# An RWKV-7 recurrence: values centred beforehand, a norm over whole tiles, and the log decay summed in two halves

## The chip, the cores and the metric

The kernel runs on one core of a Trainium2 chip. Its engines are TensorE (PE; its weight loads are listed apart as PEld), VectorE (DVE), ScalarE (ACT), GpSimd (POOL) and SyncE (SP), which issues most transfers. Each engine works through its own instructions in the order in which they stand. The metric is the device time in microseconds (us), lower is better. A profile of one execution is available for each kernel.

## What is computed

The reference is a trunk of two layers over 256 frames of width 2048: RWKV-7 time mixing, a SwiGLU, forgetting attention, a SwiGLU, and a last norm. The change touches the RWKV-7 layer alone, with 32 heads of 64 channels:

```python
w_log = -softplus(-(w0 + tanh(xw @ w1) @ w2)) - 0.5
decay = exp(-exp(w_log))
...
S_t = S_{t-1} diag(w_t) + (S_{t-1} a_t) b_t^T + v_t k_t^T          # per head
y_t = S_t r_t
...
mu = mean(y, axis=-1); var = mean(square(y - mu), axis=-1)          # over a head's 64 channels
y = (y - mu) * rsqrt(var + GN_EPS) * lnx_g + lnx_b
y = y + sum(r * k * r_k, axis=-1) * v                               # the bonus
return (y * g) @ w_o
```

The state is linear in the values: if the mean over a head's 64 channels is taken from each `v_t`, the outputs `y_t` come out with mean zero.

## The kernel before, in words

All large products go through a stream of weights. SP loads `st` (128 x 1024), ACT rounds each 128x512 block to a high half `wh` (line 149), DVE subtracts to get the low half `wl` (line 150), and PE multiplies three times per block and row tile (lines 182 to 184, the "main" matmuls). The inputs are halved in the same way, so that three products in the reduced 32-bit format stand for one in full 32 bits.

Work that isn't such a product is written as Python generators. After each triple of main matmuls the stream takes one step of each active generator (`tick`), so that recurrence work lies between main matmuls. A scheduler then orders the instructions of each engine by their dependences and places buffers.

The RWKV-7 layer has a stage of keys, a stage of values (`v0` to `v3`, about 157 to 252 us in the profile; its results go to DRAM as `vdram`), and the recurrence stage (about 252 to 615 us) under the products for the receptance, the decay, the gates and the output. There are eight units: four groups of eight heads by two row tiles of 128 frames, each of two chunks of 64 frames. For each unit
- `prepare` turns the decay `tw` into cumulative log decays with a triangular matmul (line 571), exponentials of them (lines 586 to 590 and 599), scaled keys, transposes (lines 635 and 649, copied out at lines 643 and 654), and the chunk matrices `M` (matmul line 665, masked on DVE at line 668);
- `solve` and `merge` invert a triangular block (lines 692 to 780; matmuls at 742, 749, 759, 775);
- `chain` carries the state through the two chunks (matmuls at 820, 823, 829, 834, 836; values loaded as `sv` and `vu` by `values`);
- `post` norms the result: sum per head (line 858), squares about the mean in eight ACT steps of 64 columns with a running sum (line 867), a power on POOL (line 870), the bonus from the two chunks' `vu` (line 876), the normalising in eight ACT steps (line 882), gain, bonus and gate (lines 883 to 888), and transposes (line 896).

`tw` is made at line 946 by a tanh on ACT and at line 947 by a scale and offset on DVE. The vu buffers are four, sv two. The triangular matmul is the only one of 512 columns that runs in full 32 bits.

Of the kernel before, what the change touches and what calls it, by code (L numbers as in the profile page):

```python
# [8 lines left out]
F32 = mybir.dt.float32  # L9
# [24 lines left out]
C_ID, C_TRI, C_IND, C_M, C_E, C_B8, C_LANE, C_I8, C_CAUSAL, C_END = 0, 128, 256, 258, 386, 450, 482, 486, 550, 678  # L34
# [7 lines left out]
def constants():  # L42
# [18 lines left out]
    c[:, C_CAUSAL : C_CAUSAL + P] = np.where(s[None, :] <= s[:, None], 0.0, MASKED)  # L61
    return c
# [145 lines left out]
def hybrid_kernel(ctx, tc, const, x, a_norm_g, a_mix, a_w_rkv, a_w0, a_w1, a_w2, a_a0, a_a1, a_a2,  # L208
# [127 lines left out]
    with ExitStack() as actx:  # L336
        a1 = actx.enter_context(tc.tile_pool(name="a1", bufs=1))
        rv = actx.enter_context(tc.tile_pool(name="rv", bufs=2))
        vdram = dram.tile([T, D], F32, name="vdram")
        loraw = {}  # L340

        with ExitStack() as bctx:
# [150 lines left out]

            def early():
# [29 lines left out]
            for g in range(4):  # L524
                ps = S.gemm(f"v{g}", lhs_of(xv), ready=lambda kt: has("xv", kt))
                for t in range(2):
                    vt = rv.tile([P, 512], F32, name="rv")
                    nc.scalar.copy(vt[:, :], ps[t][:, :])
                    nc.sync.dma_start(vdram[t * P : (t + 1) * P, g * 512 : (g + 1) * 512], vt[:, :])
            S.until(lambda: not S.act and not S.pend)  # L530

        with ExitStack() as bctx:
# [4 lines left out]
            u4 = bctx.enter_context(tc.tile_pool(name="u4", bufs=4))  # L537
# [5 lines left out]
            vec, wat, rts, gts, units = {}, {}, {}, {}, {}  # L543

# [17 lines left out]
            def prepare():  # L562
                for i, (g, t) in enumerate(order):
# [22 lines left out]
                    nc.scalar.activation(W, ps[:, :], AF.Exp)  # L586
                    nc.scalar.activation(Wi[:, :], ps[:, :], AF.Exp, scale=-1.0)
                    for c in range(2):
                        for q in range(2):
                            nc.scalar.activation(wc[half[c], q:8:2], pc[half[q], c:8:2], AF.Exp)  # L590
# [8 lines left out]
                    nc.scalar.activation(Wp, Wp, AF.Exp)  # L599
# [184 lines left out]
            def values(g, t, c):  # L784

                a, b = u2.tile([P, 512], F32, name="sv"), u4.tile([P, 512], F32, name="vu")
                r0 = t * P + c * C
                for d in (a, b):
                    nc.sync.dma_start(d[half[c], :], vdram[r0 : r0 + C, g * 512 : g * 512 + 512])
                return a, b  # L790

            def chain():
                nxt = values(0, 0, 0)
                for i, (g, t) in enumerate(order):
# [10 lines left out]
                    vus = []  # L805
                    for c in range(2):
# [4 lines left out]
                        vus.append(vu)  # L811
# [38 lines left out]
                    S.add(post(i, g, t, Y, vus, bon))  # L850

            def post(i, g, t, Y, vus, bon):
# [4 lines left out]
                m8 = u1.tile([P, 8], F32, name="m8")  # L857
                nc.vector.tensor_reduce(m8[:, :], h4(Y[:, :]), AX.X, ALU.add)
# [535 lines left out]
```

## Time and profile before

| | |
|---|---|
| runs (us) | 2623.15, 2628.25, 2627.87; median 2627.87 |
| the profiled execution (us) | 2622.87 |
| its span, first to last instruction (us) | 2621.1 |
| mean granted TensorE clock | 0.997 |

The profile lists for each engine the time in which it was busy. A row "A <- B" of waits names the instruction A before which its engine was idle and what released it. The chain of work that ended last is followed back from the last instruction, at each step to what released it or to the instruction ahead on its engine. Ends of matmuls are modelled, so pieces of PE work that overlap look longer than the distance between their starts.

### The profile page before, as it was taken

How to read it: one execution, taken by the hardware profiler on the slowest of the kernel's cores; microseconds unless marked ns; L12 is line 12 of the kernel's file. 1: busy time of each engine (PE TensorE's matmuls, PEld its weight loads, DVE VectorE, ACT ScalarE, POOL GpSimd, SP SyncE). 2: the span in 40 equal slices, each digit the busy share in tenths (PEclk: the TensorE clock that was granted, in tenths of full speed). 3: DMA queues.
4: the chain of work that ended last, by engine and by line, in shares of the span. 5: the costliest groups of instructions: out<-in, count | busy, mean ns of one | idle time of the engine just before them, and what ended most of it. 6: DMA issues, size and time to landing. Idle time of an engine off the chain costs nothing.

```text
span 2621.1 us, 40943 instructions
## 1 busy us (share of the span) xinstructions
PE 2574.1 (98%) x15160; PEld 2110.4 (81%) x15160; DVE 1675.0 (64%) x2965; ACT 1481.8 (57%) x2869; POOL 92.2 (4%) x69
## 2 busy tenths in 40 slices
PE   7999999999999999999999999999999999999998
PEld 5788777778888888888888888888888888888887
DVE  7885888877555555555556677676755555555554
ACT  6665787876545454544455656555554545454444
POOL 0000010100000000000001010010000000000000
PEclk9999999999999999999999999999999999999999
DMA  6676323335666666655556666664666666665554
GB/s 193 181 212 215 111 86 102 105 114 154 192 186 192 187 192 186 192 193 192 189 190 205 201 201 185 184 203 155 188 189 189 190 188 192 187 192 190 195 193 161
DMA packets 253945, 468.46 MB, mean 179 GB/s; under 512 B 22248, under 2 KB 32696, under 8 KB 253744
## 3 DMA queue, kind: packets, MB, share of 16 engines
q1 hardware_dynamic: 250448, 463.10, 58.2%
q10 hardware_dynamic: 3136, 2.74, 0.3%
q8 instruction: 119, 1.95, 0.3%
q14 instruction: 82, 0.67, 0.1%
q0 software_dynamic: 160, 0.00, 0.0%
HBM read 457.37 MB, written 4.23 MB: 176 GB/s over the span
## 4 chain that ended last, share of the span: by engine, by line
PE 92%; ACT 4%; DVE 2%; issue 1%; DMA 1%; POOL 0%; SPq 0%; POOLq 0%; ACTq 0%; DVEq 0%
PE mm L182 28%; PE mm L184 28%; PE mm L183 28%; PE bg L997 1%; ACT xb L643 1%; PE bg L829 1%; DVE wl L150 1%; PE bg L820 1%; PE bg L665 1%; PE bg L836 1%; ACT Bs L867 1%; PE bg L312 1%; PE bg L834 1%; PE bg L823 0%; DVE xmf L376 0%
## 5 line engine op out<-in xcount | busy, mean ns | idle before, releaser
L150 DVE TENSOR_TENSOR wl<-st,wh 128x512 fp32r<-128x512 f32 (+1 forms) x1648 | 1129.8, 690 | 813.1 <-ACT wh L149 806.1
L149 ACT CAST wh<-st 128x512 fp32r<-128x512 f32 (+1 forms) x1648 | 1015.8, 622 | 952.2 <-DVE wl L150 697.3
L182 PE MATMUL mm<-wh,xb 128*128 128x512 f32 x2048 | 804.6, 393 | 0.0
L184 PE MATMUL mm<-wh,xb 128*128 128x512 f32 x2048 | 800.9, 391 | 0.0
L183 PE MATMUL mm<-wl,xb 128*128 128x512 f32 x2048 | 800.5, 391 | 0.0
L182 PEld LDWEIGHTS mm<-wh,xb 128*128 128x128 f32 x2048 | 385.0, 188 | 79.5 <-issue 3.3
L184 PEld LDWEIGHTS mm<-wh,xb 128*128 128x128 f32 x2048 | 384.8, 188 | 78.8
L183 PEld LDWEIGHTS mm<-wl,xb 128*128 128x128 f32 x2048 | 385.0, 188 | 75.9
L183 PE MATMUL mm<-wl,xa 128*128 128x512 f32 x768 | 305.3, 398 | 3.0 <-DVE wl L150 1.5
L182 PE MATMUL mm<-wh,xa 128*128 128x512 f32 x768 | 306.7, 400 | 0.0
L184 PE MATMUL mm<-wh,xa 128*128 128x512 f32 x768 | 305.0, 397 | 0.0
L184 PE MATMUL mm<-wh,hb 128*128 128x512 f32 x448 | 174.5, 390 | 0.0
L183 PE MATMUL mm<-wl,hb 128*128 128x512 f32 x448 | 174.5, 390 | 0.0
L182 PE MATMUL mm<-wh,hb 128*128 128x512 f32 x448 | 174.5, 390 | 0.0
L183 PEld LDWEIGHTS mm<-wl,xa 128*128 128x128 f32 x768 | 145.2, 189 | 33.0 <-DVE wl L150 3.2
L184 PEld LDWEIGHTS mm<-wh,xa 128*128 128x128 f32 x768 | 145.0, 189 | 30.0 <-issue 0.2
L182 PEld LDWEIGHTS mm<-wh,xa 128*128 128x128 f32 x768 | 145.4, 189 | 28.8 <-issue 1.0
L182 PEld LDWEIGHTS mm<-wh,hb 128*128 128x128 f32 x448 | 84.1, 188 | 17.5
L183 PEld LDWEIGHTS mm<-wl,hb 128*128 128x128 f32 x448 | 84.1, 188 | 17.5
L184 PEld LDWEIGHTS mm<-wh,hb 128*128 128x128 f32 x448 | 84.1, 188 | 17.3
L1181 POOL TENSOR_TENSOR n<-n,pw 128x8 f32<-128x8 f32 x24 | 47.2, 1968 | 409.0 <-DVE n L1180 409.0
L1224 ACT ACTIVATE sc<-sc,nm 128x128 f32<-128x128 f32 x64 | 28.7, 449 | 26.6 <-DVE nm L1223 26.6
(293 smaller groups left out, 1941.7 us busy)
## 6 DMA issues: line engine op xcount, KB each, us to landing
st<-in_f_w_gu_dram SPq DMA_DIRECT2D x352, 512.0 KB
st<-in_f_w_d_dram SPq DMA_DIRECT2D x176, 512.0 KB
st<-in_b_w_in_dram SPq DMA_DIRECT2D x128, 512.0 KB
st<-in_a_w_rkv_dram SPq DMA_DIRECT2D x96, 512.0 KB
st<-in_a_w_o_dram SPq DMA_DIRECT2D x32, 512.0 KB
st<-in_b_w_o_dram SPq DMA_DIRECT2D x32, 512.0 KB
cb<-cdram SPq DMA_DIRECT2D x4, 1024.0 KB
x<-in_x_dram SPq DMA_DIRECT2D x12, 256.0 KB
```

The lines of the kernel that those rows point to most:

```text
L149: nc.scalar.copy(hi[:rows, :n], st)
L150: nc.vector.tensor_tensor(lo[:rows, :n], st, hi[:rows, :n].bitcast(F32), op=ALU.subtract)
L182: nc.tensor.matmul(ps[t][:, :n], xh[:rows, c], wh, start=b == 0, stop=False)
L183: nc.tensor.matmul(ps[t][:, :n], xh[:rows, c], wl, start=False, stop=False)
L184: nc.tensor.matmul(ps[t][:, :n], xl[:rows, c], wh, start=False, stop=b == kts - 1)
L312: nc.tensor.transpose(tp[:, i * T + t * P : i * T + (t + 1) * P], src[:, t, c : c + P], ident)
L643: nc.scalar.copy(dst, tpv[half[q], :, c, :])
L665: mm(pm[c][:, h * P : (h + 1) * P], fkb[us, b * 4 + h, :], far[us, b * 4 + h, :], start=True, stop=True)
L820: mm(pb[us, hs], M[:, c * 8 + h, C : 2 * C], sv[:, hs], start=True, stop=True)
L829: mm(pu[us, hs], TT[us, h, :], vu[us, hs], start=True, stop=True)
L1181: nc.gpsimd.tensor_tensor(n8[:, :], n8[:, :], pw[:, :], op=ALU.pow)
L1224: nc.scalar.activation(sc[:, c], sc[:, c], AF.Exp, bias=nm[:, t : t + 1], accum_out=nm[:, 2 + t : 3 + t])
```

## The change

Four things change in the RWKV-7 layer; nothing after it is touched.

1. While the values are made, `centred` takes each head's mean from them and writes a second copy to DRAM, `wdram`. `chain` reads the recurrence's values from `wdram`. Since `vu` is then no longer the value that the bonus needs, `post` loads the original values from `vdram` as `vn`, and `vu` has two buffers in place of four.
2. `post` needs no mean: one square over the whole tile on ACT, a sum per head on DVE, the power on POOL, and one multiplication of the whole tile on DVE in place of eight ACT steps each for squares and normalising.
3. The log decay is summed before its constant: `tw` stays the tanh, and its scale and offset move into the scale and a bias column (`dec`, four new columns of the constants) of the exponentials. Line 947 goes.
4. The triangular matmul runs as two matmuls in the reduced format, on a high half `th` (cast on ACT) and a low half `tl` (subtraction on DVE). They use the buffers named `k2` and `Wi`, which are free at that point of `prepare`.

```diff
+    n = s % C + 1
+    c[:, C_DEC : C_DEC + 4] = NEG_HALF_EXP * np.stack([n, -n, n - 1, 0 * n + C], 1)
...
+            def centred(vt, at):
+                v8 = vt[:, :].rearrange("p (h n) -> p h n", n=N)
+                m8 = lw.tile([P, 8], F32, name="m8")
+                nc.vector.tensor_reduce(m8[:, :], v8, AX.X, ALU.add)
+                nc.vector.tensor_scalar(m8[:, :], m8[:, :], -1.0 / N, None, op0=ALU.mult)
+                yield
+                wt = pre.tile([P, 2, T], F32, name="f2")[:, :, :].rearrange("p i n -> p (i n)")
+                nc.vector.tensor_tensor(
+                    wt.rearrange("p (h n) -> p h n", n=N), v8, m8[:, :].unsqueeze(2).broadcast_to([P, 8, N]), op=ALU.add
+                )
+                nc.sync.dma_start(wdram[at], wt)
...
+                    nc.sync.dma_start(vdram[at], vt[:, :])
+                    S.add(centred(vt, at))
...
+            tri = g1.tile([P, P], F32R, name="tri")
+            nc.vector.tensor_copy(tri[:, :], cst[:, C_TRI : C_TRI + P])
+            dec = cst[:, C_DEC : C_DEC + 4]
...
+                    th = u1.tile([P, 512], F32R, name="k2")
+                    tl = u1.tile([P, 512], F32R, name="Wi")
+                    nc.scalar.copy(th[:, :], tw[:, :])
+                    nc.vector.tensor_tensor(tl[:, :], tw[:, :], th[:, :].bitcast(F32), op=ALU.subtract)
                     ps = yield from S.take()
                     pc = yield from S.take()
-                    mm(ps[:, :], cst[:, C_TRI : C_TRI + P], tw[:, :], start=True, stop=True)
+                    yield
+                    mm(ps[:, :], tri[:, :], th[:, :], start=True, stop=False)
+                    mm(ps[:, :], tri[:, :], tl[:, :], start=False, stop=True)
...
-                    nc.scalar.activation(W, ps[:, :], AF.Exp)
-                    nc.scalar.activation(Wi[:, :], ps[:, :], AF.Exp, scale=-1.0)
+                    nc.scalar.activation(W, ps[:, :], AF.Exp, scale=NEG_HALF_EXP, bias=dec[:, 0:1])
+                    nc.scalar.activation(Wi[:, :], ps[:, :], AF.Exp, scale=-NEG_HALF_EXP, bias=dec[:, 1:2])
...
-                a, b = u2.tile([P, 512], F32, name="sv"), u4.tile([P, 512], F32, name="vu")
+                a, b = u2.tile([P, 512], F32, name="sv"), u2.tile([P, 512], F32, name="vu")
...
+                vn = u1.tile([P, 512], F32, name="vn")
+                nc.sync.dma_start(vn[:, :], vdram[t * P : (t + 1) * P, g * 512 : (g + 1) * 512])
...
-                for h, hs in enumerate(hsl):
-                    nc.scalar.activation(y2[:, hs], Y[:, hs], AF.Square, bias=m8[:, h : h + 1], accum_out=r8[:, h : h + 1])
+                nc.scalar.activation(y2[:, :], Y[:, :], AF.Square)
...
+                nc.vector.tensor_reduce(r8[:, :], h4(y2[:, :]), AX.X, ALU.add)
...
-                    nc.vector.tensor_tensor(
-                        h4(y2[vs, :]), h4(vus[c][vs, :]), bon[vs, :].unsqueeze(2).broadcast_to([C, 8, N]), op=ALU.mult
-                    )
+                nc.vector.tensor_tensor(h4(y2[:, :]), h4(vn[:, :]), b8(bon[:, :]), op=ALU.mult)
...
-                for h, hs in enumerate(hsl):
-                    nc.scalar.activation(Y[:, hs], Y[:, hs], AF.Identity, scale=r8[:, h : h + 1], bias=m8[:, h : h + 1])
+                nc.vector.tensor_tensor(h4(Y[:, :]), h4(Y[:, :]), b8(r8[:, :]), op=ALU.mult)
...
-                    nc.vector.tensor_scalar(a[:, :], a[:, :], NEG_HALF_EXP, NEG_HALF_EXP, op0=ALU.mult, op1=ALU.add)
```

The scheduler puts all engines' instructions into a new order. Three places follow; line numbers are those of each kernel, and of lines that both have the new numbers are 3 higher in the weight stream and 29 higher in the recurrence up to `values`.

ACT, where `post` of the first unit meets `prepare` and `merge` of later ones (Bs, r, m, Y: the norm's tiles; Xs: merge's copies; 643 and 654 `prepare`'s copies; 149 weight casts). Before:

```order
L149 CAST wh<-st 128x512
L845 COPY Y<-bg 64x512
L743 COPY Xs<-bg 128x256
L867 ACTIVATE Bs,r_3893<-Y,m_3748 128x64 x7
L743 COPY Xs<-bg 128x256
L867 ACTIVATE Bs,r_3893<-Y,m_3748 128x64
L643 COPY xb_2534<-bg 64x4x64 x8
L654 COPY WW<-bg 64x4x128 x4
```

ACT at the second unit's `post` in the changed kernel (887 the whole-tile square, 594 the cast of the high half of a later unit, 772, 672 and 683 what were 743, 643 and 654):

```order
L872 COPY Y<-bg 64x512
L973 ACTIVATE ta_4551<-mm 128x512
L887 ACTIVATE Bs<-Y 128x512
L152 CAST wh<-st 128x512
L948 COPY gt_4765<-mm 128x512
L594 CAST k_4561<-tw_4492 128x512
L152 CAST wh<-st 128x512
L772 COPY Xs<-bg 128x256
L152 CAST wh<-st 128x512
L606 ACTIVATE rr<-kk 128x512
L772 COPY Xs<-bg 128x256
L672 COPY xb_2581<-bg 64x4x64 x8
```

Eight steps ahead of the copies of `prepare` have become one, further ahead of them, and a cast has come in.

PE at the third unit's triangular matmul (665 the chunk matrices of the unit before, 759 and 775 `merge`, 820 the first matmul of `chain`). Before:

```order
L665 MATMUL bg<-xb_2535,WW 128x128 x7
L759 MATMUL bg<-Ti,xb_2534 32x32 x16
L665 MATMUL bg<-xb_2535,WW 128x128 x8
L571 MATMUL bg<-tw_3322,cst 128x512
L573 MATMUL bg<-cst,tw_3322 128x2 x4
L775 MATMUL bg<-Tt,Xs 32x32 x16
L820 MATMUL bg<-sv,xb_2534 64x64 x8
```

The same place in the changed kernel (694 was 665, 602 was 573, 804 was 775, 847 was 820; k and Wi are the high and the low half):

```order
L694 MATMUL bg<-xb_2581,WW 128x128 x11
L599 MATMUL bg<-k_3462,tri 128x512
L600 MATMUL bg<-Wi,tri 128x512
L804 MATMUL bg<-Tt,Xs 32x32 x5
L602 MATMUL bg<-cst,tw_3380 128x2 x4
L804 MATMUL bg<-Tt,Xs 32x32 x11
L186 MATMUL mm<-wl,xa_1478 128x512
L847 MATMUL bg<-sv,xb_2580 64x64 x8
```

The two matmuls stand where the one stood, with `merge` and `chain` behind them.

DVE in the changed kernel, ahead of the masks (697, formerly 668) whose results end the fifth unit's `prepare`; 595 makes the low half of the sixth unit:

```order
L595 TENSOR_TENSOR Wi<-tw_4494,k_5091 128x512
L604 TENSOR_TENSOR kk<-x_475,vk 128x512
L153 TENSOR_TENSOR wl<-st,wh 128x512 x2
L900 TENSOR_TENSOR Bs<-vn,bon 128x512
L780 TENSOR_TENSOR Ti<-bg,Ti 128x256
L901 TENSOR_TENSOR Bs<-Bs,vb 128x512
L782 STREAM_TRANSPOSE Tt<-Ti 128x256
L153 TENSOR_TENSOR wl<-st,wh 128x512
L903 TENSOR_TENSOR Y<-Y,r_5013 128x512
L697 TENSOR_TENSOR xb_2580<-bg,cst 128x512 x2
```

DVE at the same point of the first unit, where it makes the low half of the second:

```order
L697 TENSOR_TENSOR xb_2580<-bg,cst 128x512 x2
L153 TENSOR_TENSOR wl<-st,wh 97x512
L595 TENSOR_TENSOR Wi<-tw_2800,k_3059 128x512
L697 TENSOR_TENSOR xb_2580<-bg,cst 128x512 x2
L622 TENSOR_REDUCE n_3124<-rr 128x8
L614 TENSOR_TENSOR WW<-bg,tw_2800 128x512
```

And DVE before, at the masks that end the fifth unit's `prepare`:

```order
L601 SCALAR_TENSOR_TENSOR k_5212<-ta_4512,va 128x512
L751 TENSOR_TENSOR Ti<-bg,Ti 128x256
L602 SCALAR_TENSOR_TENSOR k_5212<-k_5212,x_474 128x512
L753 STREAM_TRANSPOSE Tt<-Ti 128x256
L668 TENSOR_TENSOR xb_2534<-bg,cst 128x512 x2
L869 TENSOR_SCALAR r_5047<-r_5047 128x8
L668 TENSOR_TENSOR xb_2534<-bg,cst 128x512 x2
L585 TENSOR_TENSOR WW<-bg,tw_4440 128x512
```

The subtraction is new ahead of the masks in the one unit and between them in the other, and the norm's whole-tile products (900 to 903) stand ahead of masks.

## Rows read from the trace of the kernel before

**Rows 1.** The page: span, and busy time of each engine with its share.

```profile
span 2621.1 us, 40943 instructions
...
PE 2574.1 (98%) x15160; PEld 2110.4 (81%) x15160; DVE 1675.0 (64%) x2965; ACT 1481.8 (57%) x2869; POOL 92.2 (4%) x69
```

**Rows 2.** Windows: stretch, busy PE, PEld, DVE, ACT, POOL, clock, DMA share, GB/s.

```profile
157.00:180.00 23.00, 22.42 (x122) 18.51 (x121) 19.54 (x41) 14.73 (x32) 1.59 (x5) 1.00 0.85 240
180.00:203.00 23.00, 23.00 (x103) 19.09 (x102) 11.64 (x18) 10.50 (x19) 1.59 (x1) 1.00 0.92 263
...
252.00:615.00 363.00, 347.87 (x4885) 274.96 (x4884) 291.04 (x624) 277.84 (x698) 34.95 (x25) 0.99 0.35 107
...
660.00:1400.00 740.00, 739.98 (x3338) 611.15 (x3337) 409.30 (x611) 370.10 (x612) 3.49 (x6) 1.00 0.63 190
```

**Rows 3.** Waits of PE, 250 to 645: us, times, longest; 8 of 12 rows.

```profile
PE bg L649 <- ACT xb L643: 2.7, 5, 0.8
PE bg L665 <- ACT WW L654: 2.3, 6, 1.0
PE bg L742 <- issue: 1.7, 1, 1.7
PE mm L183 <- issue: 1.5, 1, 1.5
PE bg L573 <- DVE xb L668: 1.4, 1, 1.4
PE bg L635 <- issue: 1.3, 1, 1.3
PE bg L896 <- DVE Y L888: 1.0, 1, 1.0
...
PE bg L820 <- issue: 0.3, 1, 0.3
```

**Rows 4.** The chain of work, 240 to 650 and 340 to 560: shares by line.

```profile
by line: PE mm L184 14.0%; PE mm L183 13.9%; PE mm L182 13.6%; ACT xb L643 4.5%; PE bg L829 4.2%; PE bg L820 3.7%; PE bg L665 3.7%; PE bg L836 3.6%; ACT Bs L867 3.5%; issue 3.3%; PE bg L834 3.2%; PE bg L823 3.1%; ACT WW L654 2.0%; ACT TT L7
...
by line: PE mm L184 8.9%; PE mm L182 8.7%; PE mm L183 8.4%; ACT xb L643 6.5%; PE bg L829 5.8%; PE bg L820 4.9%; PE bg L836 4.9%; PE bg L823 4.4%; ACT Bs L867 4.2%; PE bg L665 4.2%; PE bg L834 4.0%; ACT TT L769 3.6%; ACT Y L882 3.5%; issue 3
```

**Rows 5.** Timeline around 377 us: start, length, engine, instruction, idle before and releaser.

```profile
376.77 0.19 ACT L867 ACTIVATION_READ_ACCUMULATOR Bs<-Y,m 128x1 f32 x1
...
377.73 3.02 ACT L643 COPY xb<-bg 64x256 f32<-64x256 f32 x8
...
379.28 0.66 PE L649 MATMUL bg<-cst,xb 128*128 128x128 f32 x4 [0.76 <-ACT xb L643]
```

**Rows 6.** ACT groups, 252 to 615, and L1016 of the page: count | busy, mean ns.

```profile
L882 ACT ACTIVATE Y<-Y,m,r 128x64 f32<-128x64 f32 x64 | 22.4, 428 | 1.7 <-DVE m L880 1.6
L867 ACT ACTIVATE Bs<-Y,m 128x64 f32<-128x64 f32 x64 | 21.4, 338 | 2.3 <-DVE m L859 2.3
...
L577 ACT ACTIVATE rr<-kk 128x512 f32<-128x512 f32 x7 | 4.4, 627 | 1.2 <-DVE kk L575 1.1
...
L946 ACT ACTIVATE tw<-mm 128x512 f32<-128x512 f32 x8 | 4.6, 600 | 0.4 <-PE mm L184 0.3
...
L1016 ACT ACTIVATE silu<-mm,rst 128x512 f32<-128x512 f32 x44 | 29.9, 690 | 1.2
```

**Rows 7.** DVE groups, 252 to 615, same columns.

```profile
L876 DVE TENSOR_TENSOR Bs<-vu,bon 64x512 f32<-64x512 f32 x16 | 10.9, 682 | 0.2
L858 DVE TENSOR_REDUCE m<-Y 128x8 f32<-128x512 f32 x8 | 5.4, 680 | 6.9 <-ACT Y L845 6.8
L616 DVE TENSOR_TENSOR kk<-kk,n 128x512 f32<-128x512 f32 x7 | 4.8, 689 | 3.0 <-POOL n L595 3.0
L947 DVE TENSOR_SCALAR tw<-tw 128x512 f32<-128x512 f32 x8 | 3.1, 415 | 0.0
```

**Rows 8.** Pieces of the chain of work in order of time: start us, us, what.

```profile
258.55 0.86 PE bg L571 x2
...
314.68 1.06 PE bg L571 x2
...
393.28 0.23 PE mm L182
```

More of the change, by code (lines that the diff above doesn't have):

```diff
@@ L339, in hybrid_kernel @@
         vdram = dram.tile([T, D], F32, name="vdram")
+        wdram = dram.tile([T, D], F32, name="wdram")
         loraw = {}
@@ L585, in prepare @@
                     nc.vector.tensor_tensor(Wp, ps[:, :], tw[:, :], op=ALU.subtract)
-                    nc.scalar.activation(W, ps[:, :], AF.Exp)
-                    nc.scalar.activation(Wi[:, :], ps[:, :], AF.Exp, scale=-1.0)
+                    nc.scalar.activation(W, ps[:, :], AF.Exp, scale=NEG_HALF_EXP, bias=dec[:, 0:1])
+                    nc.scalar.activation(Wi[:, :], ps[:, :], AF.Exp, scale=-NEG_HALF_EXP, bias=dec[:, 1:2])
                     for c in range(2):
                         for q in range(2):
-                            nc.scalar.activation(wc[half[c], q:8:2], pc[half[q], c:8:2], AF.Exp)
+                            nc.scalar.activation(wc[half[c], q:8:2], pc[half[q], c:8:2], AF.Exp, scale=NEG_HALF_EXP, bias=dec[half[q], 3:4])
                     S.give(2)
@@ L598, in prepare @@
                     yield
-                    nc.scalar.activation(Wp, Wp, AF.Exp)
+                    nc.scalar.activation(Wp, Wp, AF.Exp, scale=NEG_HALF_EXP, bias=dec[:, 2:3])
                     k2 = u1.tile([P, 512], F32, name="k2")
@@ L784, in values @@
             def values(g, t, c):
-                a, b = u2.tile([P, 512], F32, name="sv"), u4.tile([P, 512], F32, name="vu")
+                a, b = u2.tile([P, 512], F32, name="sv"), u2.tile([P, 512], F32, name="vu")
                 r0 = t * P + c * C
                 for d in (a, b):
-                    nc.sync.dma_start(d[half[c], :], vdram[r0 : r0 + C, g * 512 : g * 512 + 512])
+                    nc.sync.dma_start(d[half[c], :], wdram[r0 : r0 + C, g * 512 : g * 512 + 512])
                 return a, b
@@ L862, in post @@
                 yield
-                yield
-                y2 = u1.tile([P, 512], F32, name="Bs")
                 r8 = u1.tile([P, 8], F32, name="r8")
-                for h, hs in enumerate(hsl):
-                    nc.scalar.activation(y2[:, hs], Y[:, hs], AF.Square, bias=m8[:, h : h + 1], accum_out=r8[:, h : h + 1])
-                yield
+                nc.vector.tensor_reduce(r8[:, :], h4(y2[:, :]), AX.X, ALU.add)
                 nc.vector.tensor_scalar(r8[:, :], r8[:, :], 1.0 / N, 64e-5, op0=ALU.mult, op1=ALU.add)
                 nc.gpsimd.tensor_tensor(r8[:, :], r8[:, :], pw[:, :], op=ALU.pow)
+                for _ in range(6):
+                    yield
                 yield
@@ L873, in post @@
                 yield
-                for c in range(2):
-                    vs = half[c]
-                    nc.vector.tensor_tensor(
-                        h4(y2[vs, :]), h4(vus[c][vs, :]), bon[vs, :].unsqueeze(2).broadcast_to([C, 8, N]), op=ALU.mult
-                    )
+                nc.vector.tensor_tensor(h4(y2[:, :]), h4(vn[:, :]), b8(bon[:, :]), op=ALU.mult)
                 nc.vector.tensor_tensor(y2[:, :], y2[:, :], vb[:, :], op=ALU.add)
-                nc.vector.tensor_tensor(m8[:, :], m8[:, :], r8[:, :], op=ALU.mult)
-                for h, hs in enumerate(hsl):
-                    nc.scalar.activation(Y[:, hs], Y[:, hs], AF.Identity, scale=r8[:, h : h + 1], bias=m8[:, h : h + 1])
+                yield
+                nc.vector.tensor_tensor(h4(Y[:, :]), h4(Y[:, :]), b8(r8[:, :]), op=ALU.mult)
                 nc.vector.tensor_tensor(Y[:, :], Y[:, :], vg[:, :], op=ALU.mult)
```

15 lines of the change are left out of this document (5 added, 10 removed).

## The prediction

> **What bounds the kernel now.** I read the page first: the span is 2621.1 us and TensorE (PE) is busy for 98% of it [rows 1]. A stage without recurrence work shows what full supply looks like: from 660 to 1400 us PE is busy for 739.98 of 740 us. In the recurrence, 252 to 615 us, it is busy for 347.87 of 363 us, so 15.1 us are idle, while VectorE (DVE) works 291.04 us and ScalarE (ACT) 277.84 us [rows 2]. These two helpers are at 80% and 77% there, and the change touches both. The idle time is named by the waits of PE: ACT ended 6.6 us of it (2.7 and 2.3 us by its PSUM copies of `prepare`, 1.6 us in small rows), DVE 2.9 us (1.4 us the masks, 1.0 us the last gate product, 0.5 us a small row), and 4.8 us was released by nothing that the profile shows [rows 3]. The chain of waits gives a second, larger figure: of the 410 us from 240 to 650, 3.5% (14.4 us) lead through the squares of the norm, line 867, and of the 220 us from 340 to 560, 3.5% (7.7 us) through the normalising steps of line 882 [rows 4]. The chain leads through an engine even where PE meanwhile does other work; it is the upper bound of what relief can give, the waits are nearer to what it does give.
>
> One burst shows the mechanism. The last steps of line 867 hold ACT's queue to 377 us; the copies of line 643 start at 377.73 us behind them, and the transposes of line 649 on PE start late at 379.28 us after 0.76 us idle for those copies [rows 5].
>
> **The change part by part, per unit (there are eight).**
>
> ScalarE. Removed: eight squares and eight normalising steps, 21.4/8 = 2.7 us and 22.4/8 = 2.8 us. Added: one whole-tile square (0.63 us, as line 577's), the cast of the decay's high half (taken as the same 0.63 us), and a bias from a column for seven exponentials. For that the nearest rows are line 946 with constants, 0.600 us, and line 1016 with a scale from a column, 0.690 us: 0.09 us each, 0.6 us in all [rows 6]. Net -3.6 us, -29 us over the kernel, which takes ACT in the stretch from 277.84 to about 249 us. What this is worth is the PE idle time behind it. Lower bound 0, if the waits that remain are made of the copies themselves (lines 643 and 654, which stay). Upper bound 22 us, the 14.4 and 7.7 us of the chain [rows 4]. I take three quarters of the 9.5 us that ACT and DVE ended [rows 3]: **-7.1 us**: PE must have idled to gain, so I stay by the waits, and not all of them stand behind a burst. The 1.0 us at the last gate product is among it: the last norm loses two bursts of 2.7 us ahead of it and gains one product.
>
> VectorE. Removed: two half-tile products of line 876 (1.36 us), the sum of line 858 (0.68 us), the scaling of line 947 (0.42 us), and two steps of 128x8. Added: the subtraction that makes the low half, the sum of the squares, a whole-tile bonus product and the scaling by the norm, at 0.68 to 0.69 us each by lines 858 and 616 [rows 7]: 2.75 us for at least 2.46 us, so at most +0.3 us. DVE stays at 80% and I count 0.
>
> TensorE. The triangular matmul of line 571 is two pieces that take 0.86 to 1.06 us of the chain; a matmul of the new kind, 128x512 as the main ones, takes 0.23 us there [rows 8]. Two of them cost 0.46 us, so 0.40 to 0.60 us are saved; at 0.46 us this is **-3.7 us** over the eight units, bounds -3.2 and -4.8. It counts in full, since nothing covers PE.
>
> The halves are a new dependency: tanh, cast on ACT, subtraction on DVE, matmul. Where the subtraction stands ahead of the masks of the unit before, as the order shows for the sixth unit, the cover is those masks and the norm's products, and I count 0. Without that cover one unit pays cast plus subtraction, 1.3 us, 10.5 us in all. In the second and the last unit it stands between the masks; there PE's matmul on the low half, and behind it lines 804 and 847, can wait for it: 0.69 us each, **+1.4 us**, bounds 0 and 10.5.
>
> Centred values. In the value stage DVE gets a sum and a difference per tile, 0.68 + 0.69 us, 11 us in all. Only the first tile pair meets a busy DVE (19.54 of 23 us from 157 to 180 us); from 180 to 203 us it is 11.64 of 23 us [rows 2]. The cover is DVE's idle time; I count 0, and 3 us, the pair's work, if the last rows of the low-rank product wait for it there.
>
> Transfers. 256 KB more are written per tile and 256 KB read back by `post`, 4.2 MB; two value buffers go, so each load of `vu` waits for the chunk before the last, as `sv` does already. The value stage moves 263 GB/s at 0.92 of the engines' time where it is fullest, the recurrence only 107 GB/s at 0.35 [rows 2]. The first loads of `sv` and `vu` leave that fullest stretch, which pays for the new writes. SyncE's queue can be held by a `wdram` write or a `vn` load, and behind it stand the weight loads; in the recurrence DMA is two thirds free. 0, upper bound 3 us for one late weight block.
>
> The sum: -7.1 - 3.7 + 1.4 = -9.4 us. The profiled execution took 2622.87 us, so 2613.5 us by its own scale; the median of the runs shown, 2627.87 us, is 5.0 us above it, so **2618 us** (2618.5) by the median. About 0.2%, 5.3 us, is what a measurement here can tell from no change.
>
> **Rivals.**
>
> Only the matmul counts (chance 0.21). ACT was not late, the copies of `prepare` were, and they stay: the waits of lines 649 and 665 stand there again, and only 3.7 us go: 2624.2 us, -0.14%, the same. For it: the 5.0 us of those two rows are half of what ACT and DVE ended [rows 3]. Against it: the copies start late behind a burst in the one shown [rows 5].
> The Trainium skill ("Perfetto Trace Analysis", Identifying the Most-Contended Engine) says that one improves a kernel by improving its most contended engine; ACT is not that here, and by this rule the time would be this rival's. The trace agrees for the kernel as a whole and bears less on the 363 us in which ACT and DVE end waits of PE.
>
> The whole chain counts (0.18). Behind each burst the weight casts, copies and value steps all run late, and the pieces under lines 867 and 882 go with the matmul's part: 14.4 + 7 + 3.7 - 1.4 = -24 us, 2604 us. For it: the share of the chain; against it: only 15.1 us of idle time on record.
>
> The halves become the wait (0.10). DVE at 80% is late with the subtraction, or ACT's cast waits at the head of its queue for DVE to free the buffer named k2; then copies and weight casts queue behind it. In front of PE's first matmul of the chain this costs 1.3 us or more a unit. It decides from 10.8/8 = 1.35 us a unit on; with 2 us a unit it is +16 - 10.8 = +5 us, 2633 us, slower. For it: DVE works 291.04 of 363 us, and PE has waited 1.4 us for its masks at just this place [rows 2, 3]. Against it: the order sets the subtraction well ahead in the sixth unit.
>
> **How the numbers follow.** The forecast has 0.48, the three rivals 0.21, 0.18 and 0.10, and 0.03 is left for a stall elsewhere in the new order. From the forecast's own bounds (waits -3 to -10, matmul -3.2 to -4.8, halves 0 to +5) its range is 2611 to 2626 us. The range of 8 in 10 takes in the first rival and half of the second and a mild case of the third: **2604 to 2631 us**. Faster by over 0.2% are most of the forecast and all of the second rival: 0.64. Within 0.2%: the first rival and the forecast's weak end, 0.24. Slower: 0.12.
>
> **What would show it.** Line 571 gone and two matmuls of 0.23 us in its place; ACT's busy time between 252 and 615 us down by some 29 us; DVE's there unchanged and 11 us more before 252 us; PE's idle time in the stretch from 15.1 to about 8 us, with the waits of lines 649 and 896 (their new numbers) shorter; no PE wait on the low half above 0.7 us; the stages after 660 us as long as before. I am wrong if a wait behind the casts or the subtraction appears in every unit, if the idle time stays near 15 us, or if the value stage grows.

## The result, and the profile after

| | before | after |
|---|---|---|
| median of six runs each, us | 2625.75 (2623.07 to 2629.85) | 2634.95 (2631.14 to 2641.78) |
| profiled execution, us | 2622.87 | 2641.78 |
| its mean granted clock | 0.997 | 0.994 |

The changed kernel is slower: the ratio is 1.0036, 95% interval 1.0021 to 1.005, some 9 us more, where 2618 us (range 2604 to 2631 us), some 9 us less, had been predicted. The page of the profiled execution, to set beside [rows 1]:

```profile
span 2640.0 us, 40839 instructions
...
PE 2589.2 (98%) x15160; PEld 2114.4 (80%) x15160; DVE 1681.7 (64%) x2974; ACT 1453.2 (55%) x2693; POOL 92.1 (3%) x69
```

ACT works 28.6 us less, as meant, and PE is busy 15 us longer with as many instructions. Of the 19 us by which the span grew, waiting makes only 4 (2640.0 less 2589.2 us is 50.8, before 47.0); PE's own instructions became slower somewhere. The windows of the same stretches as in [rows 2], and of one stage of the recurrence:

```profile
157.00:180.00 23.00, 22.34 (x121) 18.68 (x121) 21.09 (x47) 13.87 (x30) 0.00 (x0) 1.00 0.76 238
180.00:203.00 23.00, 23.00 (x103) 19.04 (x102) 13.77 (x24) 11.57 (x20) 0.00 (x0) 1.00 0.88 277
252.00:615.00 363.00, 345.14 (x4858) 274.92 (x4857) 285.78 (x601) 247.35 (x516) 35.60 (x25) 0.97 0.37 113
660.00:1400.00 740.00, 739.16 (x3297) 606.34 (x3295) 405.69 (x606) 367.71 (x609) 3.51 (x6) 1.00 0.62 189
...
420.00:510.00 90.00, 83.81 (x1311) 67.39 (x1309) 70.39 (x153) 65.15 (x143) 9.29 (x7) 0.91 0.37 109
```

Three things are to be seen. In the recurrence ACT fell from 277.84 to 247.35 us and DVE hardly moved, but PE's idle time did not fall: 17.9 us against 15.1. There the granted clock is 0.97 over the stretch and 0.91 from 420 to 510 us, so part of it ran at the lower level, 1.2 GHz; before it was 0.99. And from 660 to 1400 us, where not a line of the code changed, PE is as full as before and does 3,297 matmuls instead of 3,338.

When the main matmuls of the two traces are laid beside each other in their order, the one at 252 us stands 0.3 us earlier than before, the one at 660 us 5.5 us later, and the last 19.0 us later. So 13.5 us of the profiled pair were lost behind the recurrence. But for one step that is 1.0 us longer (at 1387 us of before, at the start of the attention stage), they came evenly, in three places: while the down products of either feed-forward stage read hb, and in the attention stage. Groups of matmuls on hb, first in the kernel before, then in the changed one (count, busy time, mean ns):

```profile
L184 PE MATMUL mm<-wh,hb 128*128 128x512 f32 x448 | 174.5, 390 | 0.0
```

```profile
L187 PE MATMUL mm<-wh,hb 128*128 128x512 f32 x448 | 177.2, 396 | 0.0
```

Matmuls overlap, so the mean time of one is longer than the step from one to the next. The step is seen in a stretch that holds nothing else, the windows of hb alone (the view counts only instructions on hb, so ACT and DVE stand at 0), before and after:

```profile
1279.00:1309.00 30.00, 30.00 (x134) 24.84 (x134) 0.00 (x0) 0.00 (x0) 1.00 0.57 193
```

```profile
1287.00:1317.00 30.00, 30.00 (x130) 24.18 (x129) 0.00 (x0) 0.00 (x0) 1.00 0.57 190
```

30 us by 134 is 224 ns, by 130 it is 231 ns, both at the full granted clock. Taken over all of them, from one start to the next, it is 226.7 ns before and 233.3 ns after: 6.6 ns by 1,344 matmuls are 8.9 us.

In the recurrence the waits of PE, to set beside [rows 3]:

```profile
PE bg L771 <- issue: 3.0, 2, 2.3
PE bg L778 <- issue: 2.7, 2, 2.1
PE mm L186 <- DVE wl L153: 1.7, 1, 1.7
PE bg L788 <- ACT xb L672: 1.6, 4, 0.4
PE mm L185 <- ACT tw L967: 1.1, 1, 1.1
...
PE bg L599 <- ACT k L594: 0.7, 1, 0.7
```

The copies of `prepare` (now line 672, and 683 for WW) end less of the idle time than lines 643 and 654 did, and other waits stand in their place. ACT ended 6.6 us of it before and 6.5 us now, DVE 2.9 and 3.0 us (sums over the rows of the same view, 252 to 615 us).

### The profile page after: what moved, and what is told of

Its sections match the earlier page's. It is cut to its first block, busy times and chain, and to the rows that moved or that the text cites. A ratio compares the mean times of both kernels' runs of the same rounds, so it can differ in the third digit from the quotient of the medians.

```text
span 2640.0 us, 40839 instructions
## 1 busy us (share of the span) xinstructions
PE 2589.2 (98%) x15160; PEld 2114.4 (80%) x15160; DVE 1681.7 (64%) x2974; ACT 1453.2 (55%) x2693; POOL 92.1 (3%) x69
## 4 chain that ended last, share of the span: by engine, by line
PE 85%; ACT 2%; DVE 1%; issue 1%; DMA 0%; POOL 0%; POOLq 0%; ACTq 0%; DVEq 0%
PE mm L185 26%; PE mm L186 26%; PE mm L187 26%; PE bg L1017 1%; PE bg L847 1%; PE bg L856 1%; ACT xb L672 1%; PE bg L315 1%; PE bg L850 1%; PE bg L694 1%; PE bg L863 1%; PE bg L861 0%; PE bg L1253 0%; ACT WW L683 0%; PE bg L771 0%
## 5 line engine op out<-in xcount | busy, mean ns | idle before, releaser
L187 PE MATMUL mm<-wh,hb 128*128 128x512 f32 x448 | 177.2, 396 | 0.0
L185 PE MATMUL mm<-wh,hb 128*128 128x512 f32 x448 | 177.2, 395 | 0.0
```

What stands on the lines that cost most here:

```text
L185: nc.tensor.matmul(ps[t][:, :n], xh[:rows, c], wh, start=b == 0, stop=False)
L187: nc.tensor.matmul(ps[t][:, :n], xl[:rows, c], wh, start=False, stop=b == kts - 1)
```

## The experiments

Each time below is a median over 10 to 12 runs, with exceptions named; before, run beside them, had medians of 2625.0 to 2627.8 us. Since runs of one kernel differ most in the granted clock, the table also splits the mean: the clock's part is (1 - granted clock) x span of each run, and the rest is what is left of its time. For before the rest is 2614 us in every batch (2613.8 to 2614.6) with a clock's part of 12 to 14 us; most of the difference between its runs, 2619 to 2633 us in the first batch, goes with the clock's part (0.92 us for 1 us).

| run | median us | ratio to before, 95% interval | clock's part | rest |
|---|---|---|---|---|
| the change (6 runs) | 2634.95 | 1.0036 [1.0021, 1.005] | 12.7 | 2623.3 |
| dead_columns | 2638.15 | 1.0036 [1.0023, 1.005] | 11.0 | 2626.6 |
| hb_alone_shifted | 2634.12 | 1.0033 [1.0018, 1.0048] | 12.3 | 2622.8 |
| padded_after (64 bytes) | 2635.23 | 1.003 [1.0017, 1.0043] | 14.1 | 2621.6 |
| after_128 | 2632.81 | 1.0031 [1.0017, 1.0045] | 14.3 | 2619.9 |
| all_aligned (128 bytes) | 2633.81 | 1.0033 [1.0019, 1.0047] | 13.2 | 2621.5 |
| after_256 | 2624.79 | 0.9995 [0.9978, 1.0012] | 14.4 | 2611.5 |
| after_512 | 2625.03 | 0.9996 [0.9983, 1.0008] | 15.5 | 2610.7 |
| all_moved_128 | 2625.8 | 0.999 [0.9971, 1.0009] | 14.4 | 2611.1 |
| weights_moved_128 (4 runs) | 2668.69 | 1.0152 [1.0124, 1.0179] | 10.7 | 2657.0 |
| norm_alone | 2623.1 | 0.9992 [0.9979, 1.0005] | 13.1 | 2611.5 |
| halves_alone (5 runs) | 2648.31 | 1.0081 [1.0066, 1.0096] | 23.8 | 2625.5 |
| halves_cast_on_dve | 2633.32 | 1.0019 [1.0005, 1.0033] | 21.9 | 2610.6 |
| after_512_no_halves | 2625.54 | 1.0002 [0.999, 1.0015] | 14.9 | 2611.5 |
| after_512_cast_on_dve | 2627.79 | 1.0003 [0.9991, 1.0014] | 18.4 | 2609.5 |

### Is it where the tiles lie?

The change adds four columns to the constants tile. In SBUF, the on-chip memory from which the engines read, the tiles of every stage, hb and the extra weight buffers of the attention stage among them, are placed behind it; the weight buffers, xa and xb lie ahead of it and stay where they were. The built program shows what that does: hb of the first feed-forward stage starts at byte 161,408 of each partition before and at 161,440 after (four columns are 16 bytes, and places are rounded up to 32). The simplest test is the kernel before with four columns that nothing reads.

```diff
-... C_CAUSAL, C_END = 0, 128, 256, 258, 386, 450, 482, 486, 550, 678
+... C_CAUSAL, C_END = 0, 128, 256, 258, 386, 450, 482, 486, 550, 682
```

> The kernel before with four more columns in the constants tile that nothing reads (682 instead of 678); the computation is whole. Theory A (placement): the tile grows by 32 bytes a partition as it is rounded up, and every tile that is placed behind it moves from an address that is a multiple of 64 to one that is 32 past it, hb and the extra weight buffers of the attention stage among them. The 1,344 matmuls that read hb should then take 233 instead of 227 ns, as in the changed kernel, 8.9 us in all, with some 3.4 us more in the attention stage: about 12 us more than before, ratio 1.0047, near 2638 us. Theory B (the later stages slow for another reason that comes with the change, the second DRAM tile or its transfers; the rest is the recurrence's clock): four unread columns do nothing, ratio 1.000, 2626 us.

Measured: 2638.15 us, ratio 1.0036, 12.1 us more without the clock's part. The matmuls on hb, in the groups by line:

```profile
L184 PE MATMUL mm<-wh,hb 128*128 128x512 f32 x448 | 177.2, 396 | 0.0
```

It is the row of the changed kernel to the digit. Theory A holds and B falls: unread bytes alone cost all that the change lost. Next, hb by itself, with 32 unread bytes ahead of its two tiles.

```diff
+            gap = hp.tile([P, 8], F32, name="gap")
             hb = [hp.tile([P, 28, T], F32R, name=f"hb{i}") for i in range(2)]
```

> The kernel before with an unread tile of 32 bytes a partition ahead of the two hb tiles of each feed-forward stage; nothing else moves, and the computation is whole. Theory A2: the 1,343 matmuls on hb take 233 instead of 227 ns, 8.9 us, and the attention stage is unchanged: 2623.4 us without the clock's part, near 2636 us, ratio 1.0034. Rival (placement costs through the weights or the constants and not through hb, or through all tiles together): the matmuls stay at 227 ns and the time at 2627 us, ratio 1.000.

Measured: ratio 1.0033; 8.2 us more without the clock's part (8.9 expected), the step of a matmul on hb 233.3 ns, the attention stage as long as before. So hb carries two thirds of the loss. The other third, some 4 us, falls in the attention stage, where the extra weight buffers moved with it. There the weights go round nine buffers, two of them the extra ones. A block feeds six matmuls. From one start to the next, where no other work lies between, three blocks in a row of each round of nine take 231 to 232 ns a matmul in dead_columns and the other six 228; in before and in hb_alone_shifted all nine take 227 to 228 ns. That speaks for the extra buffers; why it is three blocks and not two isn't shown.

### Which places are good ones?

The changed kernel, with the constants tile padded so that what lies behind it moves by 64, 128, 256 and 512 bytes against before.

```diff
-..., C_CAUSAL, C_DEC, C_END = 0, 128, 256, 258, 386, 450, 482, 486, 550, 678, 682
+..., C_CAUSAL, C_DEC, C_END = 0, 128, 256, 258, 386, 450, 482, 486, 550, 678, 694
```

(694 columns for 64 bytes; 710, 742 and 806 for 128, 256 and 512.)

> The changed kernel with the constants tile padded to 694 columns, 12 of them unread, so that what lies behind it moves by 64 bytes instead of 32; the computation is whole. Theory A: hb matmuls back at 227 ns, the stages after the recurrence as long as before, 12 to 13 us less than the changed kernel: 2622.5 us, ratio 0.9988 to before; what is left is what the change itself does in the recurrence, between -7 and 0 us. Theory B: no difference to the changed kernel, 2635 us, ratio 1.0036. A mixed result, about 2629 us, would mean that the recurrence loses by itself (its granted clock was at half for 24 us, against 7 us before).

> The changed kernel with the constants tile padded to 710 columns, so that what lies behind it moves by 128 bytes; the computation is whole. For each run the time lost to the clock is (1 - granted clock) x span; what is left is 2614.5 us on average for before, 2626.6 with the dead columns, 2623.3 for the changed kernel, 2621.6 with 64 bytes of padding. Theory A2 (hb and the extra weight buffers must start at a multiple of 128 bytes): hb matmuls at 227 ns, the stages after the recurrence as long as before, 2611 us without the clock's part, and with 12 to 14 us for the clock 2624 us, ratio 0.999. Rival (no multiple but the old addresses themselves, or another distance between tiles, decide): 233 ns again and 2635 us, ratio 1.003.

> The changed kernel with the constants tile padded to 742 columns: hb and the extra weight buffers move by 256 bytes against before; the computation is whole. Shifts of 32, 64 and 128 bytes gave 233.3, 233.3 and 232.3 ns for a matmul on hb, no shift 226.7. In the kernel before, every tile that the main matmuls read (weights, xa, xb, hb, the extra weight buffers) starts 128 bytes past a multiple of 512. Theory P512 (the two operands are read without loss only at the same place within 512 bytes): 256 bytes are out of step too, about 231 to 233 ns and 2633 us, ratio 1.003. Theory P256 (the same place within 256 bytes is enough): 227 ns and 2624 us, ratio 0.999.

> The changed kernel with the constants tile padded to 806 columns: everything behind it moves by 512 bytes against before; the computation is whole. By P512 and P256 alike: hb matmuls at 227 ns, the stages after the recurrence as long as before, 2611 us without the clock's part and 12 to 14 us for the clock, 2624 us, ratio 0.999. If the matmuls stay at 233 ns, the distance between the tiles or the whole address decides, and the time stays at 2634 us, ratio 1.003.

Measured: 64 bytes gave nothing back (233.3 ns, 1.003), which Theory A in its first form, a multiple of 64 bytes, had got wrong; 128 bytes next to nothing (232.4 ns, 1.0031), so A2 fell as well. 256 and 512 bytes gave it all back: 226.7 ns, ratios 0.9995 and 0.9996. P256 it is. The same group and the same stretch of hb alone in after_256:

```profile
L187 PE MATMUL mm<-wh,hb 128*128 128x512 f32 x448 | 174.3, 389 | 0.0
```

```profile
1281.00:1311.00 30.00, 30.00 (x134) 24.86 (x133) 0.00 (x0) 0.00 (x0) 1.00 0.57 193
```

In between stood a run with every small tile of the recurrence and the attention stage padded to 128 bytes as well, on top of after_128:

```diff
-                    n8 = u1.tile([P, 8], F32, name="n8")
+                    n8 = u1.tile([P, 32], F32, name="n8")[:, 0:8]
...
```

> The changed kernel with 710 constant columns and every small tile of the recurrence and of the attention stage padded to 128 bytes, so that all large tiles there start at a multiple of 128 bytes (in the kernel before many start 32, 64 or 96 past one); the computation is whole. If misplaced operands cost time in the recurrence and the attention as they do at hb, this is shorter than the run after_128, by up to 5 us (some 4,000 small PE instructions in the recurrence, 1 ns or so each): 2619 us, ratio 0.997. If only matmuls of 512 columns or weights of 128x128 that are read again and again feel it, no difference to after_128: 2624 us, ratio 0.999.

Measured: 1.0033, as after_128. It rested on the rule of 128 bytes, and says only that that rule brings nothing elsewhere.

What was open then is whether the address decides or the place of a matmul's two operands against each other. Two unread tiles tell them apart, on after_256: one ahead of the weight buffers moves everything, and a second one behind them moves all but the weights back into step with 256 bytes.

```diff
         self.stage = ctx.enter_context(tc.tile_pool(name="stage", bufs=self.NS))
+        ctx.enter_context(tc.tile_pool(name="gap", bufs=1)).tile([P, 32], F32, name="gap")
         self.wp = ctx.enter_context(tc.tile_pool(name="wp", bufs=self.NW))
+        ctx.enter_context(tc.tile_pool(name="gap2", bufs=1)).tile([P, 32], F32, name="gap2")
```

(all_moved_128 has the first added line, weights_moved_128 both.)

> As after_256, with an unread tile of 128 bytes ahead of the weight buffers, so that weights, xa, xb, hb and the extra weight buffers all move by another 128 bytes together and start at a multiple of 256, where before they start 128 past one; the computation is whole. Theory R (what counts is that the two operands of a matmul lie at the same place within 256 bytes): no change to after_256, 227 ns, 2625 us, ratio 0.9995. Theory S (the address itself must lie 128 past a multiple of 256): all 9,840 main matmuls take 5 to 7 ns more, some 55 us, 2680 us, ratio 1.02.

> As all_moved_128, with a second unread tile of 128 bytes behind the weight buffers: the weights alone start at a multiple of 256, all else 128 past one as before; the computation is whole. Theory R: every main matmul on these weights is out of step, 232 instead of 227 ns, some 9,300 of 9,840, about 50 us, 2675 us, ratio 1.02. Theory S for the loaded operand alone (xa, xb, hb must lie 128 past a multiple of 256, the streamed one anywhere): no change, 2625 us, ratio 0.9995.

Measured: moving all together changes nothing (0.999), moving the weights alone costs 1.5%: 2668.69 us, 46 us more than all_moved_128 without the clock's part, 5 ns for each of the 9,300 or so matmuls on those buffers (50 us expected). Theory R holds, S falls. First the group on hb in all_moved_128, the same as that of after_256 above, and a group on xb in after_256:

```profile
L188 PE MATMUL mm<-wh,hb 128*128 128x512 f32 x448 | 174.3, 389 | 0.0
```

```profile
L185 PE MATMUL mm<-wh,xb 128*128 128x512 f32 x2048 | 803.5, 392 | 0.0
```

Then both groups in weights_moved_128, where their lines stand 2 further down than in after_256. hb lies 512 bytes behind its old place there, which after_512 showed to be harmless; with the weights out of step it is slow again (232.4 ns a step, as at the same distance in after_128), and so is xb, which had been fast in every run until then (227.1 ns, here 232.4).

```profile
L187 PE MATMUL mm<-wh,xb 128*128 128x512 f32 x2048 | 813.7, 397 | 0.0
...
L189 PE MATMUL mm<-wh,hb 128*128 128x512 f32 x448 | 176.8, 395 | 0.0
```

### What is the change worth by itself?

The norm and the centred values alone, in the kernel before, constants as they were:

```diff
+                S.add(centred(vt, at))
...
-                for h, hs in enumerate(hsl):
-                    nc.scalar.activation(y2[:, hs], Y[:, hs], AF.Square, bias=m8[:, h : h + 1], accum_out=r8[:, h : h + 1])
+                nc.scalar.activation(y2[:, :], Y[:, :], AF.Square)
...
```

> The kernel before with the values and the norm alone changed: centred values written in the value stage, whole-tile square, sum, bonus and scaling, two value buffers less; the decay as before. The constants tile keeps 678 columns, so the stages after the recurrence keep their addresses. The computation is whole. By the prediction's term: PE waits behind ACT bursts fall by 7.1 us, 2618.6 us, ratio 0.9973. Rival (relief on ACT buys nothing, the waits are the copies themselves): 2626 us, ratio 1.000. Third (the norm's new order costs in the recurrence: new waits, or PE granted half its clock more often): 2630 us or more, ratio above 1.0015.

Measured: 2623.1 us, ratio 0.9992, an interval that holds 1; 3.0 us less without the clock's part, not 7.1. The recurrence and the waits in it:

```profile
252.00:615.00 363.00, 349.93 (x4880) 276.52 (x4879) 292.69 (x611) 244.80 (x517) 34.08 (x25) 0.98 0.38 114
```

```profile
PE bg L775 <- DVE Ti L767: 2.7, 2, 1.5
PE bg L758 <- issue: 2.3, 2, 1.8
PE bg L681 <- ACT WW L670: 1.7, 6, 0.3
PE mm L182 <- ACT xa L917: 1.5, 1, 1.5
PE bg L665 <- ACT xb L659: 1.3, 3, 0.4
```

ACT works 33 us less than in [rows 2] and PE idles 13.1 us instead of 15.1. The waits for the copies of xb halved (2.7 to 1.3 us) and those for WW fell by a quarter (2.3 to 1.7 us), but other waits stand in their place: DVE's Ti, which is in none of before's rows, now ends 2.7 us. In sum ACT and DVE end 9.2 us of idle time, 9.5 before.

The halves alone, with the norm of before (padded by 64 bytes, which costs the later stages 11 to 12 us as in padded_after):

```diff
-                    mm(ps[:, :], cst[:, C_TRI : C_TRI + P], tw[:, :], start=True, stop=True)
+                    mm(ps[:, :], tri[:, :], th[:, :], start=True, stop=False)
+                    mm(ps[:, :], tri[:, :], tl[:, :], start=False, stop=True)
...
```

> The kernel before with the decay alone changed: the exact halves, the two matmuls in place of line 571, the scales and biases of the exponentials, the scaling of the tanh dropped; norm and values as before. The constants tile is padded to 694 columns (a shift of 64 bytes), and the triangular matrix lies in an idle scratch tile since the value buffers leave no room. The computation is whole. By the prediction's terms: -3.7 and +1.4, with its ACT casts hidden, 2.3 us less than before: 2623.5 us, ratio 0.9991. Rival (the halves become the wait): a wait of PE for the low half in each unit, more than 1 us each, and 2630 us or more, ratio 1.002.

Measured: 2648.31 us, ratio 1.0081. Its mean is 22.6 us above that of before: 11.6 us are clock (its runs had granted clocks of 0.990 to 0.992), and the 11.0 us that are left are what the placement costs, so at the full clock the halves bring 1 us at most. The wait for the low half in each unit that the rival foresaw isn't there: of PE's waits from 252 to 615 us one names the high half (1.4 us) and none the low one. Windows of its profile, a stretch at the full clock and two at the lower level (0.50 is 1.2 GHz):

```profile
330.00:348.00 18.00, 16.78 (x365) 13.40 (x364) 15.13 (x33) 9.68 (x30) 2.25 (x2) 1.00 0.29 87
349.00:365.00 16.00, 15.81 (x120) 12.10 (x119) 10.00 (x20) 13.91 (x35) 1.60 (x1) 0.50 0.26 76
...
472.00:491.00 19.00, 16.00 (x131) 14.82 (x132) 13.63 (x33) 16.84 (x41) 2.01 (x1) 0.50 0.25 75
```

And the timeline ahead of the first of the two, ACT's rows and PE's:

```profile
346.34 0.62 ACT L152 CAST wh<-st 128x512 fp32r<-128x512 f32 x1 [1.24 <-DMA st<-in_a_g_dram]
346.99 2.65 ACT L656 COPY xb<-bg 64x256 f32<-64x256 f32 x7
```

```profile
346.02 0.75 PE L762 MATMUL bg<-Xs,Tt 32*32 32x32 f32 x64
348.54 1.06 PE L662 MATMUL bg<-cst,xb 128*128 128x128 f32 x4 [1.76 <-ACT xb L656]
```

ACT stands 1.24 us at the head of its queue for a weight block, its copies start late behind it, PE has only 32x32 matmuls and then idles 1.76 us, and right behind that the clock is at its lower level. That the wait and the fall belong together here is argued from this one place, and nothing in it needs the halves: in the profile of dead_columns, which has none, PE idles 2.15 us ahead of 303.9 us, and the lower level holds from 305 to 326 us. What is particular to this run is how much of its time all five executions spent there. Whether it is the cast's queue was tried: the high half cast on DVE, and hb in step with the weights this time.

```diff
-                    nc.scalar.copy(th[:, :], tw[:, :])
+                    nc.vector.tensor_copy(th[:, :], tw[:, :])
```

> The halves alone with the norm of before, as in the run halves_alone, but with the high half cast on DVE instead of ACT and with hb and the weight buffers at their old addresses (two small tiles are merged to make room); the computation is whole. The run halves_alone lost 23.8 us to the clock against 12.2 for before and, without the placement's 12.1 us, was 1.1 us shorter than before at full clock. Theory C (the cast in ACT's queue, between the norm's bursts and the copies of prepare, makes PE stall, and the stalls bring the low clock): the cast off ACT gives the clock back, 2613.5 + 12 = 2626 us, ratio 1.000. Rival D (the dependency tanh, cast, subtraction, matmul stalls PE wherever the cast runs): the clock still loses 20 us or more, 2636 us or more, ratio 1.003 or more.

Measured: 2633.32 us, ratio 1.0019. Without the clock's part it is 4.0 us faster than before, but the clock takes 21.9 us. Theory C falls. Of D, the 20 us lost to the clock came, its time (2636 us or more) did not, and its reason isn't shown: no row of PE's waits in the profile of this run, 252 to 615 us, names either half. In both orders that were tried, the halves with the norm of before bring more of the low clock; why stays open. With the new norm and the cast on ACT they hardly do (15.5 us against 14.9 without them):

```diff
-                    mm(ps[:, :], tri[:, :], th[:, :], start=True, stop=False)
-                    mm(ps[:, :], tri[:, :], tl[:, :], start=False, stop=True)
+                    mm(ps[:, :], cst[:, C_TRI : C_TRI + P], tw[:, :], start=True, stop=True)
...
```

> As after_512, without the halves: one triangular matmul in full precision on the raw tanh, as line 571 before; scales and biases of the exponentials as in the change, so the computation is whole. What the halves bring under the new norm is the difference to after_512. By the prediction's terms (-3.7 and +1.4) this run is 2.3 us longer than after_512: 2626.5 us, ratio 1.000. By the run norm_alone (2611.5 us without the clock's part) the two are equal: 2624 us, ratio 0.999. If the halves cost the clock under the new norm too, this run is shorter, by up to 10 us: 2614 to 2620 us, ratio 0.996.

> As after_512, with the high half cast on DVE instead of ACT; the computation is whole. In the runs with the norm of before, that cast on DVE left 2610.6 us without the clock's part, on ACT 2613.4 us (2625.5 less the placement's 12.1), so 2.8 us are to be had if they carry over to the new norm: 2608.5 us and 13 us for the clock, 2621.5 us, ratio 0.998. If the cast was dear only between the old norm's ACT bursts, no difference to after_512: 2624 us, ratio 0.999.

Measured: without the halves 2625.54 us, with them (after_512) 2625.03, with their cast on DVE 2627.79: 0.8 us in favour of the halves without the clock's part, and nothing that the intervals tell apart. The cast on DVE brought 1.2 us of the 2.8 expected without the clock's part, and lost 2.9 to the clock (18.4 us, where before, run beside it, lost 13.4).

No version beats before beyond its interval. Nearest are all_moved_128 (0.999) and norm_alone (0.9992); after_256 is what the change would have been with its constants padded, 10 us below the change as it was made.

## Why the prediction was wrong

**The missing term.** The sum, "-7.1 - 3.7 + 1.4", had no term for the place of other tiles, and "the stages after 660 us as long as before" was written down as a sign of being right. That step failed, and with it the sentence ahead of the prediction that nothing after the RWKV-7 layer is touched, which is so for instructions and not for addresses: the four columns of `dec` put hb and the extra weight buffers out of step with the weights, +12 us (2626.6 less 2614.5 in dead_columns). It alone turns the 3 us that the change gains without the clock's part (after_256 2.4, after_512 3.2 us, against before run beside them) into 9 us lost (2623.3 against 2614.5, with nearly the same clock's part). The four new columns were known (item 3 of the change); none of my rivals, the one of 0.03 for "a stall elsewhere in the new order" included, had it.

**"I take three quarters of the 9.5 us that ACT and DVE ended: -7.1 us."** The mechanism was half right and the size wrong. ACT's load fell as worked out (-29 us; measured 277.84 to 247.35), and the waits behind its bursts did get shorter. But in norm_alone the idle time that ACT and DVE end came to 9.2 us: by the rows, PE waited elsewhere in the same chain of copy, matmul, mask and transpose instead, above all for DVE's Ti. The runs give 3.0 us (norm_alone) and 2.4 us (after_512_no_halves) for the whole norm. Most of what ACT gave up was slack: its weight casts wait 24.8 us for PE's matmuls in the new trace, 13.6 us before. The rival "only the matmul counts" stood on this, and the Trainium skill's rule ("Perfetto Trace Analysis", Identifying the Most-Contended Engine) with it; the runs agree with the rule: 30 us off an engine that is not the contended one were worth a tenth of that. Of the rival itself only this half came true: the matmul's 3.7 us did not show either (below).

**"Two of them cost 0.46 us."** In the second unit they do (0.45 us from start to start); in four of the eight they cost 0.65 to 0.66 us. Two pieces of the chain of waits, to compare with [rows 8], and the timeline of PE at the same place:

```profile
354.49 0.43 PE bg L599
354.92 0.23 PE bg L600
```

```profile
354.42 0.50 PE L599 MATMUL bg<-k,tri 128*128 128x512 f32 x1
354.76 0.40 PE L600 MATMUL bg<-Wi,tri 128*128 128x512 f32 x1
355.09 0.69 PE L804 MATMUL bg<-Tt,Xs 32*32 32x32 f32 x32
```

From start to start the two take 0.34 and 0.33 us, where they take 0.23 us each in the second unit. There the pair stands behind main matmuls and ahead of another of 128 rows; here it stands between matmuls on 64 rows (line 694) and on 32 (line 804). The old full-precision matmul shows the same: its first piece took 0.53 us behind matmuls on 64 rows, 0.43 us behind main ones. So the neighbours cost it, and not the new format. Against the 0.86 to 1.06 us of before, 0.2 to 0.4 us a unit are saved, 1.6 to 3.2 us in all instead of 3.7; the runs show 0.8 us for the halves as a whole (after_512 against after_512_no_halves), which the scatter does not tell from nothing.

**"+1.4 us" for the halves.** The place was wrong and the size near: no row of PE's waits names the low half, and the high half of the first unit cost 0.7 us. The rival "the halves become the wait" did not come true: with the old norm the halves did cost time (halves_cast_on_dve, 1.0019), but through the clock, and no wait of PE for the low half was found.

**What was right.** DVE unchanged (291.04 to 285.78 us). The value stage counted at 0: DVE does 1.55 and 2.13 us more in the two windows of [rows 2] and 8.1 us up to 252 us (11 had been counted), and the matmul at 252 us is no later. The transfers at 0: the fullest stretch went from 263 to 277 GB/s and PE stayed full.

**The clock.** The profiled pair differs by 19 us, the medians by 9. About 8 us of the former are the clock of two single executions: (1 - 0.994) x 2640.0 is 15.8 us, (1 - 0.997) x 2621.1 is 7.9 us. Over its six runs, the change as made took no more of it than before did (12.7 against 12 to 14 us). With padded constants it took somewhat more than before run beside it, 0.7 to 2.4 us in each of the six such runs from padded_after to all_moved_128 in the table: 14.4 against 13.4 us in after_256, 15.5 against 13.4 in after_512. Each difference lies within the scatter, but all have one sign; it seems that the clock takes back part of what the change gains without it.

Put together from the runs: +12 for the place, -3 for the norm, -1 for the halves: +8 without the clock's part, and +8.8 was measured (2623.3 less 2614.5). With the tiles in step the change would have been within 0.1% of before (after_256, after_512). That is nearest to the first rival by its number alone: it had the matmul gain 3.7 us and the norm nothing, and the runs give the norm 2.4 to 3.0 us and the halves 0.8.

Two things stay open: why halves and old norm together lose 10 us more to the clock, and why a distance within 256 bytes matters at all. The latter is shown by timing, its mechanism isn't.

## What to carry to other kernels

A small tile that grows moves every tile behind it, so after any change of a size, compare the step of matmuls in stages whose code did not change, before explaining the stage that did. Keep the loaded and the streamed operand of the main matmuls at the same place within 256 bytes; here that was worth 12 us to 46 us, more than the change aimed at. And where engines wait for each other in turn, take relief on an engine that is not the bound at what the next link lets through, not at what the waits that name it add up to.

## What the hardware showed that was not expected

- The step of a 128x512 matmul depends on where its operands lie against each other: 226.7 ns when they start at the same byte within 256, 232.4 ns at a distance of 128, 233.3 ns at 32 and 64. The address itself does not matter (all_moved_128, 226.7 ns).
- Runs of one kernel on one chip, 2619 to 2633 us for before in the first batch, differ mostly by the share of time at the lower of TensorE's two clocks. With (1 - granted clock) x span taken off, the spread of before's runs falls from 4.3 to 4.9 us in the four batches to 1.3 to 1.5 us (one standard deviation), and differences of 3 us between kernels can be read.
